# A batched row gather on Trainium2: eight resident 2 MB blocks in place of four rotating 0.5 MB buffers

## The chip, the core and the metric

The kernel runs on one core of one Trainium2 chip. The core has several engines, each with its own instruction queue: PE (matrix multiply), DVE (vector), ACT (scalar), POOL (GpSimd) and SP (sync). It has 16 DMA engines, which move data between the chip's main memory (HBM) and the core's own memory (SBUF, 128 partitions). DMAs are issued from the queues of SP, ACT and POOL. The metric is the device time of one execution in microseconds (us); lower is better.

## The reference

For each of 32 batches, 128 rows of 1024 float32 values (4 KB each) are picked out of 512 rows by an index:

```python
x = np.random.randn(32, 512, 1024).astype(np.float32)
indices = np.random.randint(0, 512, (32, 128)).astype(np.int32)

for b in range(32):
    result[b] = x[b, indices[b]]
```

Nothing is computed beyond the row addresses. 16.78 MB are read and 16.78 MB written. On the device the indices are 64-bit integers, so each one is 8 bytes long.

## The kernel before

The indices are loaded transposed, so that partition n holds index n of each of the 32 batches (L15, issued on SP). In the memory they lie batch by batch, so every element of this load is a run of 8 bytes. DVE copies the low halves of the 64-bit numbers into 32-bit ones (L17). POOL writes an iota that holds 512 b in column b (L20), and DVE adds the two (L21): column b is then the row number, in x seen as one table of 32 x 512 rows, that each partition is to fetch for batch b.

Then a loop runs over the 32 batches. POOL issues an indirect DMA (a gather, L27): partition n receives the 4 KB row that its row number names, 0.5 MB for the batch. A plain DMA stores the buffer to the output (L31), issued on SP for even batches and on ACT for odd ones. The buffers come from a pool with four slots, so gather b + 4 reuses the space of gather b, and waits until the store of batch b has landed. The framework sets all waits. It has eight semaphores for DMAs that POOL issues and eight for those of SP and ACT, used in turn; DMASW0 to DMASW7 are those of POOL's gathers in the order listings below, DMAHW0 to DMAHW7 those of loads and stores.

The order of the work on each queue is the order of the program. POOL runs 32 gathers, SP the index load and 16 stores, ACT 16 stores.

Of the kernel before, what the change touches and what calls it, by code (L numbers as in the profile page):

```python
# [5 lines left out]


@with_exitstack
def kernel(ctx, tc, x, indices, out):
    nc = tc.nc  # L10
    B, S, D = x.shape
    N = indices.shape[1]
    tp = ctx.enter_context(tc.tile_pool(name="sbuf", bufs=4))
    idx = tp.tile([128, B], dtype=indices.dtype)
    nc.sync.dma_start(out=idx[:], in_=indices[:, :].rearrange("b n -> n b"))  # L15
    idx32 = tp.tile([128, B], dtype=mybir.dt.int32)
    nc.vector.tensor_copy(out=idx32[:], in_=idx[:].bitcast(mybir.dt.int32)[:, ::2])  # L17
    idx2 = tp.tile([128, B], dtype=mybir.dt.int32)
    iota = tp.tile([128, B], dtype=mybir.dt.int32)
    nc.gpsimd.iota(iota[:], pattern=[[S, B]], base=0, channel_multiplier=0)  # L20
    nc.vector.tensor_tensor(out=idx2[:], in0=idx32[:], in1=iota[:], op=mybir.AluOpType.add)  # L21
    xf = x.flatten_outer_dims()
    of = out.flatten_outer_dims()
    engs = [nc.gpsimd, nc.sync, nc.scalar]
    for b in range(B):
        buf = tp.tile([N, D], dtype=x.dtype)
        nc.gpsimd.indirect_dma_start(  # L27
            out=buf[:], out_offset=None,
            in_=xf[:], in_offset=bass.IndirectOffsetOnAxis(ap=idx2[:, b:b+1], axis=0),
        )  # L30
        engs[1 + b % 2].dma_start(out=of[b*N:(b+1)*N], in_=buf[:])  # L31


# [1 line left out]
_INS = ['x', 'indices']  # L35
_OUTS = [((32, 128, 1024), 'float32')]


def kernel(**inputs):
    import numpy as _np  # L40
    import concourse.bacc as _bacc
    import concourse.tile as _tile
    from concourse import mybir as _mybir
    from concourse.bass_utils import run_bass_kernel_spmd as _run

    nc = _bacc.Bacc("TRN2", target_bir_lowering=False, num_devices=1)  # L46
    arrays, args = {}, []
    for name in _INS:
        a = _np.ascontiguousarray(inputs[name])
        if a.dtype.kind in "iu":  # L50
            a = a.astype(_np.int64)
        arrays[f"in_{name}_dram"] = a
        args.append(nc.dram_tensor(f"in_{name}_dram", a.shape, _mybir.dt.from_np(a.dtype), kind="ExternalInput").ap())
    for i, (shape, dtype) in enumerate(_OUTS):
        dt = _mybir.dt.from_np(_np.dtype(dtype))
        args.append(nc.dram_tensor(f"out_{i}_dram", shape, dt, kind="ExternalOutput").ap())
    with _tile.TileContext(nc) as tc:  # L57
        kernel(tc, *args)
    r = _run(nc, [arrays], core_ids=[0])
    got = tuple(r.results[0][f"out_{i}_dram"] for i in range(len(_OUTS)))  # L60
    return got[0]
```

## Time and profile before

| | |
|---|---|
| Median of 3 timed runs | 110.75 us (109.97 to 112.1) |
| Span of the profiled execution, the only time given of it | 109.6 us |
| POOL busy | 30.5 us (28%) |
| DVE busy | 0.4 us |
| Gathers (POOL, L27) | 32, 944 ns each on POOL, 6.1 us from issue to landing (median) |
| Stores (L31) | 16 on SP (5.7 us to landing), 16 on ACT (5.0 us) |
| Index load | 32 KB, 4.0 us to landing |
| Bytes through the DMA engines | 33.60 MB, 307 GB/s on average over the span |

How to read it: the busy time of POOL is what it takes to write the descriptors of the gathers; the data move later, on the DMA engines. The DMA share in a stretch is the time that packets took there, divided by 16 engines and by the length of the stretch. A packet that waits for its data counts as busy. The rate in GB/s counts a byte once for each DMA that moves it, so the 16.78 MB count twice, as gather and as store. One queue, q0, has the gathers; q1 and q10 have the DMAs of SP and ACT.

### The profile page before, as it was taken

The page shows a single profiled execution, that of the slowest core. Times are in us where ns is not written, and L with a number is a line of the kernel's source. Part 1 is how long each engine was busy: PE and PEld are TensorE (multiplying, and loading weights), DVE is VectorE, ACT ScalarE, POOL GpSimd, SP SyncE. Part 2 cuts the span into 40 slices and gives each one's busy share as a digit, 9 for nine tenths or more (in the row PEclk, how much of TensorE's full clock was granted, in tenths as well). Part 3 has the DMA queues.
Part 4 walks back from the last instruction along what each step waited for, and adds up shares of the span by engine and source line. Part 5 has one row for each costly group of instructions (what it writes and reads, how often), then busy time and mean ns, then how long its engine had stood idle before and what let it go on. Part 6 is the DMA issues. An engine that isn't in the chain of part 4 may idle for free.

```text
span 109.6 us, 173 instructions
## 1 busy us (share of the span) xinstructions
DVE 0.4 (0%) x2; POOL 30.5 (28%) x37
## 2 busy tenths in 40 slices
DVE  0100000000000000000000000000000000000000
POOL 1076002730057002730067002730037200660000
DMA  3429899899998889999998999798997999898991
GB/s 5 7 34 332 217 362 417 272 309 321 422 375 294 262 341 426 300 293 333 423 390 257 366 413 414 221 342 206 419 387 247 326 329 416 293 365 263 405 401 55
DMA packets 13329, 33.60 MB, mean 307 GB/s; under 512 B 5136, under 2 KB 5136, under 8 KB 13328
## 3 DMA queue, kind: packets, MB, share of 16 engines
q0 software_dynamic: 4608, 16.78, 48.3%
q1 hardware_dynamic: 6416, 8.42, 20.8%
q10 hardware_dynamic: 2304, 8.39, 18.7%
q14 instruction: 1, 0.01, 0.0%
HBM read 16.81 MB, written 16.78 MB: 306 GB/s over the span
## 4 chain that ended last, share of the span: by engine, by line
DMA 78%; issue 7%; POOL 2%; POOLq 1%; DVE 0%; DVEq 0%
DMA out_dram<-buf 41%; DMA buf<-in_x_dram,idx 34%; DMA idx<-in_indices_dram 4%; POOL buf L27 2%; POOLq L57 1%; DVE idx L21 0%; DVE idx L17 0%; POOLq L27 0%; DVEq L21 0%
## 5 line engine op out<-in xcount | busy, mean ns | idle before, releaser
L27 POOL DMA_INDIRECT buf<-in_x_dram,idx x32 | 30.2, 944 | 67.1 <-DMA out_dram<-buf 54.7
L20 POOL IOTA iota<- 128x32 int32 x1 | 0.1, 146 | 0.4 <-PEq L57 0.4
L17 DVE COPY idx<-idx 128x32 int32<-128x32 int32 x1 | 0.2, 181 | 4.8 <-DMA idx<-in_indices_dram 4.8
L21 DVE CUSTOM_DVE_ANT_0 idx<-idx,iota 128x64 uint16<-128x64 uint16 x1 | 0.2, 192 | 0.1
L46 POOL MEMSET const-float32-0.0<- 128x1 f32 x1 | 0.1, 99 | 0.2 <-issue 0.2
L46 POOL MEMSET const-uint8-127<- 128x1 uint8 x1 | 0.1, 119 | 0.0
L46 POOL MEMSET const-bfloat16-1.0<- 128x1 bf16 x1 | 0.1, 113 | 0.0
L46 POOL MEMSET const-float32-1.0<- 128x1 f32 x1 | 0.1, 105 | 0.0
## 6 DMA issues: line engine op xcount, KB each, us to landing
out_dram<-buf SPq DMA_DIRECT2D x16, 512.0 KB, 5.7
out_dram<-buf ACTq DMA_DIRECT2D x16, 512.0 KB, 5.0
buf<-in_x_dram,idx POOLq DMA_INDIRECT x32, 6.1
idx<-in_indices_dram SPq DMA_DIRECT2D x1, 32.0 KB, 4.0
```

Of the source, the lines that this page charges most:

```text
L17: nc.vector.tensor_copy(out=idx32[:], in_=idx[:].bitcast(mybir.dt.int32)[:, ::2])
L20: nc.gpsimd.iota(iota[:], pattern=[[S, B]], base=0, channel_multiplier=0)
L21: nc.vector.tensor_tensor(out=idx2[:], in0=idx32[:], in1=iota[:], op=mybir.AluOpType.add)
L27: nc.gpsimd.indirect_dma_start(out=buf[:], out_offset=None, in_=xf[:], in_offset=bass.IndirectOffsetOnAxis(ap=idx2[:, b:b+1], axis=0),)
L46: nc = _bacc.Bacc("TRN2", target_bir_lowering=False, num_devices=1)
L57: with _tile.TileContext(nc) as tc:
```

## The change

The batches are taken in eight blocks of four. Partition p = 32 c + q (c from 0 to 3, q from 0 to 31) handles batch 4 g + c of block g, and there the four consecutive output rows 4 q to 4 q + 3. A block is a tile of 128 partitions x 4096 floats (16 KB in each partition); the four rows lie beside each other in it. Gather k of a block fetches row 4 q + k of every partition, so one gather touches four batches, 32 rows of each. There are still 32 gathers of 0.5 MB. When the four gathers of a block have landed, one DMA stores it: 2 MB that are contiguous in the output, 16 KB from each partition. Stores alternate between SP and ACT by block. All eight blocks have a space of their own (128 KB in each partition), and none is used twice.

The index load follows the new layout: each partition reads, for each block, a run of four indices (32 bytes). The offset of the batch, 512 (4 g + c), is made from an iota, with 512/32 = 16 added from one partition to the next; a bitwise-and clears its low nine bits. One DVE instruction adds the low halves of the indices to it directly; the copy is gone.

```diff
-    tp = ctx.enter_context(tc.tile_pool(name="sbuf", bufs=4))
-    idx = tp.tile([128, B], dtype=indices.dtype)
-    nc.sync.dma_start(out=idx[:], in_=indices[:, :].rearrange("b n -> n b"))
-    idx32 = tp.tile([128, B], dtype=mybir.dt.int32)
-    nc.vector.tensor_copy(out=idx32[:], in_=idx[:].bitcast(mybir.dt.int32)[:, ::2])
-    idx2 = tp.tile([128, B], dtype=mybir.dt.int32)
-    iota = tp.tile([128, B], dtype=mybir.dt.int32)
-    nc.gpsimd.iota(iota[:], pattern=[[S, B]], base=0, channel_multiplier=0)
-    nc.vector.tensor_tensor(out=idx2[:], in0=idx32[:], in1=iota[:], op=mybir.AluOpType.add)
+    P = nc.NUM_PARTITIONS
+    K = 4
+    G = B // K
+    per = N // K
+    const = ctx.enter_context(tc.tile_pool(name="const", bufs=1))
+    rows = ctx.enter_context(tc.tile_pool(name="rows", bufs=1))
+    idx = const.tile([P, G, K], indices.dtype, name="idx")
+    nc.sync.dma_start(
+        out=idx[:], in_=indices.rearrange("(g c) (q k) -> (c q) g k", c=K, k=K)
+    )
+    ramp = const.tile([P, G * K], mybir.dt.int32, name="ramp")
+    base = const.tile([P, G * K], mybir.dt.int32, name="base")
+    nc.gpsimd.iota(
+        ramp[:], pattern=[[K * S, G], [0, K]], base=0, channel_multiplier=S // per
+    )
+    nc.vector.tensor_single_scalar(
+        out=base[:], in_=ramp[:], scalar=~(S - 1), op=mybir.AluOpType.bitwise_and
+    )
+    row = const.tile([P, G * K], mybir.dt.int32, name="row")
+    low = idx[:].rearrange("p g k -> p (g k)").bitcast(mybir.dt.int32)[:, ::2]
+    nc.vector.tensor_tensor(out=row[:], in0=low, in1=base[:], op=mybir.AluOpType.add)
     xf = x.flatten_outer_dims()
-    of = out.flatten_outer_dims()
-    engs = [nc.gpsimd, nc.sync, nc.scalar]
-    for b in range(B):
-        buf = tp.tile([N, D], dtype=x.dtype)
-        nc.gpsimd.indirect_dma_start(
-            out=buf[:], out_offset=None,
-            in_=xf[:], in_offset=bass.IndirectOffsetOnAxis(ap=idx2[:, b:b+1], axis=0),
-        )
-        engs[1 + b % 2].dma_start(out=of[b*N:(b+1)*N], in_=buf[:])
+    of = out.rearrange("(g c) (q k) d -> g (c q) (k d)", c=K, k=K)
+    for g in range(G):
+        block = rows.tile([P, K * D], x.dtype, name=f"block{g}")
+        for k in range(K):
+            c = g * K + k
+            nc.gpsimd.indirect_dma_start(
+                out=block[:, k * D:(k + 1) * D], out_offset=None,
+                in_=xf[:], in_offset=bass.IndirectOffsetOnAxis(ap=row[:, c:c + 1], axis=0),
+            )
+        eng = nc.sync if g % 2 == 0 else nc.scalar
+        eng.dma_start(out=of[g], in_=block[:])
```

What this does to POOL's queue is not in the diff, since the framework sets the waits. The order on POOL before, from the iota on, with the first gathers (the names in brackets are the semaphores that an instruction waits for):

```order
7 L20 IOTA iota_63 128x32
8 L27 DMA buf_66<-in_x_dram,idx2_62 128x1024 [waits DVE_49]
9 L27 DMA buf_69<-in_x_dram,idx2_62 128x1024
10 L27 DMA buf_72<-in_x_dram,idx2_62 128x1024
11 L27 DMA buf_75<-in_x_dram,idx2_62 128x1024
12 L27 DMA buf_78<-in_x_dram,idx2_62 128x1024 [waits DMAHW1_49,DMASW0_49]
13 L27 DMA buf_81<-in_x_dram,idx2_62 128x1024 [waits DMAHW2_49,DMASW1_49]
14 L27 DMA buf_84<-in_x_dram,idx2_62 128x1024 [waits DMAHW3_49,DMASW2_49]
```

The same place now:

```order
7 L34 IOTA ramp 128x32
8 L50 DMA block_69<-in_x_dram,row 128x1024 [waits DVE_49]
9 L50 DMA block_69<-in_x_dram,row 128x1024 x3
10 L50 DMA block_75<-in_x_dram,row 128x1024 x4
11 L50 DMA block_81<-in_x_dram,row 128x1024 [waits DMASW0_49]
12 L50 DMA block_81<-in_x_dram,row 128x1024 [waits DMASW1_49]
13 L50 DMA block_81<-in_x_dram,row 128x1024 [waits DMASW2_49]
14 L50 DMA block_81<-in_x_dram,row 128x1024 [waits DMASW3_49]
```

Before, the fifth gather is the first to wait, for a store (DMAHW1) and for the gather that filled the buffer last. Now the first eight are issued without such a wait, and the ninth waits for the first gather alone (DMASW0, whose semaphore it uses again). No gather waits for a store.

The stores on SP's queue before, after the index load:

```order
1 L15 DMA idx<-in_indices_dram 128x32x1
2 L31 DMA out_dram<-buf 128x1024 [waits DMASW0_49]
3 L31 DMA out_dram<-buf 128x1024 [waits DMASW2_49]
4 L31 DMA out_dram<-buf 128x1024 [waits DMASW4_49]
5 L31 DMA out_dram<-buf 128x1024 [waits DMASW6_49]
6 L31 DMA out_dram<-buf 128x1024 [waits DMAHW1_49,DMASW0_49]
```

And now, all of SP's DMAs:

```order
1 L27 DMA idx<-in_indices_dram 128x8x4
2 L55 DMA out_dram<-block_69 128x4096 [waits DMASW2_49,DMASW3_49,DMASW1_49,DMASW0_49]
3 L55 DMA out_dram<-block_81 128x4096 [waits DMASW2_49,DMASW3_49,DMASW1_49,DMASW0_49]
4 L55 DMA out_dram<-block_93 128x4096 [waits DMASW2_49,DMASW3_49,DMASW1_49,DMASW0_49]
5 L55 DMA out_dram<-block_105 128x4096 [waits DMASW2_49,DMASW3_49,DMASW1_49,DMASW0_49]
```

A store waited for one gather; now it waits for the four of its block. SP has four stores in place of sixteen, and ACT likewise.

## The prediction

> **What bounds the kernel now.** I read the page first, then the waits, the chain of waits, and then stretches of a few microseconds, because the page's averages mix two kinds of traffic.
>
> The page, sections 1 to 3 (engines, DMA in 40 slices, DMA queues):
>
> ```profile
> span 109.6 us, 173 instructions
> DVE 0.4 (0%) x2; POOL 30.5 (28%) x37
> DMA  3429899899998889999998999798997999898991
> GB/s 5 7 34 332 217 362 417 272 309 321 422 375 294 262 341 426 300 293 333 423 390 257 366 413 414 221 342 206 419 387 247 326 329 416 293 365 263 405 401 55
> q0 software_dynamic: 4608, 16.78, 48.3%
> ```
>
> No compute engine matters: POOL, which issues the gathers, is busy 28%. The 16 DMA engines are busy 80 to 90% of nearly every slice after the third, and yet the rate swings between 206 and 426 GB/s. So "busy" does not mean "moving at full rate". q0 carries the gathers.
>
> The waits of POOL, and the first pieces of the chain of waits (start us, us, what):
>
> ```profile
> POOL buf L27 <- DMA out_dram<-buf: 54.7, 7, 8.5
> 5.58 4.48 DMA buf<-in_x_dram,idx
> 10.06 0.02 issue
> 10.07 7.71 DMA out_dram<-buf
> 17.79 0.02 issue
> 17.81 0.02 POOLq L27
> 17.83 0.72 issue
> 18.55 5.11 DMA buf<-in_x_dram,idx
> ```
>
> There are four buffers. POOL issues four gathers, then waits until the store of the first has landed: 7 waits, 54.7 us. The chain alternates gather, store, gather. It looks like a latency problem, but POOL's idle time counts only where the DMA engines idle too. The stretches decide that. First, seven in which only gathers move (columns: stretch, length, DVE, POOL, clock, DMA share, GB/s):
>
> ```profile
> 22.00:26.00 4.00, 0.00 (x0) 0.94 (x1) 1.00 0.94 299
> 34.00:38.00 4.00, 0.00 (x0) 1.33 (x2) 1.00 0.87 296
> 47.00:51.00 4.00, 0.00 (x0) 0.92 (x1) 1.00 0.93 289
> 59.00:62.00 3.00, 0.00 (x0) 0.94 (x1) 1.00 0.86 292
> 71.00:75.00 4.00, 0.00 (x0) 1.18 (x2) 1.00 0.90 313
> 84.00:88.00 4.00, 0.00 (x0) 1.38 (x2) 1.00 0.96 333
> 96.00:100.00 4.00, 0.00 (x0) 1.88 (x2) 1.00 0.97 359
> ```
>
> Weighted by length they make 8432/27 = 312 GB/s at a mean share of 24.86/27 = 0.92. An engine that always had a gather packet would therefore work at 312/0.92 = 339 GB/s (all 16 together). Now stretches that hold only stores (18 to 20, 30 to 32, 104 to 106), and two late in a group, where stores run beside the last gather:
>
> ```profile
> 18.00:20.00 2.00, 0.00 (x0) 1.14 (x2) 1.00 0.99 404
> 30.00:32.00 2.00, 0.00 (x0) 0.94 (x1) 1.00 1.03 420
> 104.00:106.00 2.00, 0.00 (x0) 0.00 (x0) 1.00 1.01 414
> 40.00:42.00 2.00, 0.00 (x0) 0.00 (x0) 1.00 1.04 424
> 102.00:104.00 2.00, 0.00 (x0) 0.00 (x0) 1.00 1.01 416
> ```
>
> Stores alone go at about 415 GB/s, and so does a mixture. That is the point of the case: gathers alone are slow (about 312), anything with stores in it is not. And there are the worst places, at the start of a group (20 to 22, 82 to 84) and where stores have been issued but hardly move yet (12 to 14, 74 to 76):
>
> ```profile
> 20.00:22.00 2.00, 0.00 (x0) 1.68 (x2) 1.00 0.86 223
> 82.00:84.00 2.00, 0.00 (x0) 1.44 (x2) 1.00 0.71 205
> 12.00:14.00 2.00, 0.00 (x0) 0.00 (x0) 1.00 0.76 178
> 74.00:76.00 2.00, 0.00 (x0) 0.00 (x0) 1.00 0.86 188
> ```
>
> So the bound is the DMA engines' work, spoiled by low-rate stretches in every group of four.
>
> **The change, part by part.**
>
> *Head.* The index load and the ends of the span:
>
> ```profile
> q1 hardware_dynamic: 4112, 0.03, 41.4%
> 0.74 4.01 DMA idx<-in_indices_dram
> 4.78 0.19 DVE idx L17
> 5.11 0.20 DVE idx L21
> 0.00:1.80 1.80, 0.00 (x0) 0.35 (x5) 1.00 0.00 0
> 5.58:7.30 1.72, 0.00 (x0) 1.42 (x2) 1.00 0.00 0
> 108.00:109.60 1.60, 0.00 (x0) 0.00 (x0) 1.00 0.00 0
> ```
>
> The first row is the DMA view of the first 5.5 us: 4112 packets for 32 KB, nearly all of 8 bytes, keep the engines busy for 0.414 x 5.5 = 2.28 us. The new load reads runs of four indices (32 bytes), 128 x 8 = 1024 of them. At the same time for each that is 0.57 us, a saving of 1.7; the lower bound is nothing, if a 32-byte packet costs four times as much. I take 1.7, since the row's price is one of packets and not of bytes (32 KB in 2.28 us are 14 GB/s). The copy at L17 goes (5.11 - 4.78 = 0.33 us); the new bitwise-and depends only on the iota and hides under the index load (0.19 us if that cover went). First gather issue: 5.58 - 1.7 - 0.33 = 3.55. Data follow 1.72 us later: 5.3 us instead of 7.3.
>
> *Waits for the output buffer.* Each of eight blocks has its own space, so no gather waits for a store. But the order shows that a wait remains: the ninth gather and each after it waits for the gather eight places before it, whose semaphore it shares. Eight gathers stay in flight where four did. At 339 GB/s one gather lands every 0.524/339 = 1.55 us, so eight make 12 us of queue, against 4.48 us from issue to landing of the very first. Two gathers of the first group, in order of time:
>
> ```profile
> 6.97 0.94 POOL L27 DMA_INDIRECT buf<-in_x_dram,idx  x1 [0.30 <-issue]
> 8.22 0.94 POOL L27 DMA_INDIRECT buf<-in_x_dram,idx  x1 [0.30 <-issue]
> ```
>
> POOL issues one in 1.25 us, faster than one lands. The queue never runs dry; the cold starts (223, 205 GB/s) fall away after the first. With the queue full an engine that is ahead no longer waits for its neighbours, so I take 339 for gathers alone, not 312. Both ends stay for the range: 261 below, and 359, the best row, above.
>
> *Stores.* Thirty-two of 0.5 MB become eight of 2 MB, rows of 16 KB instead of 4. Each waits for four gathers. Behind a waiting store on SP or ACT stand only later stores, whose data come later anyhow; nobody else waits for them. What it costs for one store to start: the index load was issued at 0.74 us (the chain's row) and the row 0.00:1.80 shows no data until about 1.8, so 1.1 us; gathers cover that for seven of eight. For bytes I take 415 GB/s, between the two bounds 404 and 424; over the 14.7 MB of the first seven that is +0.9 or -0.8 us.
> The Trainium skill ("DMA: Bandwidth & Descriptors", Anatomy of one DMA) gives each DMA about 2.0 us fixed plus its bytes, and its Rules for kernel authors want at least 1 MiB. Twenty-four fewer stores would then save up to 48 us if each stood alone. The rows 30 to 32 and 104 to 106, with 0.5 MB stores at 420 and 414 GB/s, leave no such cost to remove: stores on two queues hide it. I take zero.
>
> *Who shares the engines.* A store row is now 16 KB; a gather row remains 4 KB. I take it that the engines alternate row by row, so that a running store has four fifths of 415 = 332 GB/s and a gather one fifth. Then stores and gathers still come in turns:
> - first block, gathers alone: 2.10/339 = 6.2 us;
> - each store: 2.10/332 = 6.3 us, in which 0.52 MB are gathered; the other 1.57 MB of the next block go alone, 1.57/339 = 4.6 us. Seven such cycles: 76.5 us;
> - the last store: nothing left to hide its start, 1.1 + 2.10/415 = 6.15 us. Before, the last store moved 0.5 MB; this longer tail is the change's own cost;
> - end of the span after the last data: 1.6 us.
>
> Sum: 5.3 + 6.2 + 76.5 + 6.15 + 1.6 = 95.7 us of span, against 109.6. The profiled execution has no time but its span; the median of the timed runs, 110.75, lies 1.1 above it, which I add: **96.8 us**.
>
> In general, with r the rate of gathers alone and 2.10 + 7 x 1.57 = 13.1 MB going alone, the time is 58.3 + 13.1/r (the 58.3 being head 5.3, seven stores 44.1, last store 6.15, end 1.6, and 1.1). At 359 GB/s it gives 94.8, at 312 100.3, at 261 108.5.
>
> **The rivals.**
>
> *B, an even mixture.* If engines alternate by equal bytes rather than by rows, a store gets half the rate and overlaps the whole next block. Then gathers are alone only in the first block: 5.3 + 6.2 + 29.4/415 (70.7) + 6.15 + 1.6 + 1.1 = 91.1 us. For it: mixed stretches already run at 424 and 416. Against: nothing of before shows a 16 KB row, so who wins a turn is open.
> The Trainium skill ("DMA: Bandwidth & Descriptors", Queues, rings and completion order) says each engine takes turns between queue rows packet by packet, and its section SWDGE vs HWDGE vs iDMA prefers packets of at most 4096 B. By that rule the turns are of equal bytes and B is what happens. No row here shows it for rows above 4 KB.
>
> *C, the gain is given back.* Gathers alone run at 240 to 261 GB/s, since the slow stretches between a store's issue and its first data are a matter of the switch and not of the buffers. By the same formula 261 gives 108.5 and 240 gives 112.9: no change. Against: seven rows between 289 and 359.
>
> *D, slower.* A deep gather queue in front of a store is itself what slows gathers. The place is the stretch between a store's issue and its first data (12 to 14: 178, 74 to 76: 188), and POOL's queue would now be eight deep there, always. At 188 GB/s it is 58.3 + 13.1/0.188 = 128 us. It decides from 240 GB/s down. For it: these stretches hold backlog and no POOL work, so lack of descriptors did not make them slow. Against: 22 to 26 and 96 to 100 have the same backlog and 299 and 359.
>
> *E, the change does not do what it says*: POOL still stalls for the gather eight places back. It does wait there, but with 12 us of work queued; it costs only if the DMA share falls between gathers. I put this within C.
>
> **How the numbers follow.** About 2% is what a measurement of this kernel can tell from no change: 108.5 to 113.0. Forecast with r from 261 up: 0.53; B: 0.22; C with E: 0.13; D: 0.12. Faster is 0.53 + 0.22 = 0.75, same 0.13, slower 0.12. The range goes from B with mixing at 424 (about 89.5) to just past the edge of the forecast, into C: 109.5. It leaves out D and most of C, about 2 in 10. The predicted time is the forecast's own, 97.
>
> **What would show it.** Head: the first gather issued near 3.6 us, index packets near 1024. No wait of POOL on out_dram. No slice below 250 GB/s between 10 and 90 us; D would show slices near 190 throughout. A against B: in A the slices swing between about 330 and 415 with gathers near a fifth of a store's stretch; in B they stand near 415 throughout and successive stores overlap. A last stretch of about 5 us with stores alone. The forecast is wrong if gathers alone stay under 261 GB/s, or if the 2 MB stores, alone, do not reach 404.

## The result and the profile after

The changed kernel takes 92.3 us (median of 4 runs, 91.6 to 92.8), against 111.4 us for the kernel before in the same comparison. The ratio is 0.834, 95% interval 0.827 to 0.841. This ratio and those below compare only the fast runs of both kernels, so they are not exactly the quotients of the medians. The forecast was 97.0 in a range of 89.5 to 109.5: the direction and the range held, and the gain was about 1.4 times the forecast's (19.1 us against 13.8).

The page of the changed kernel, sections 1 to 3 and one line of 6:

```profile
span 89.8 us, 113 instructions
DVE 0.4 (0%) x2; POOL 30.6 (34%) x37
DMA  1159999999999999999999989999999989995990
GB/s 7 7 139 321 312 367 369 412 421 436 376 418 458 421 405 423 432 434 416 411 447 425 469 358 378 467 429 387 420 494 432 431 350 414 460 445 235 467 467 0
q0 software_dynamic: 4608, 16.78, 48.2%
q1 hardware_dynamic: 1616, 8.42, 22.4%
q10 hardware_dynamic: 576, 8.39, 21.8%
block<-in_x_dram,row POOLq DMA_INDIRECT x32, 18.3
```

Two things differ from before. The DMA row is full from the fourth slice almost to the end, and the rate under it no longer falls back in every group (its lows before lay between 206 and 293); one dip, to 235, is left near the end. Also, a gather now takes 18.3 us from issue to landing where it took 6.1, and this costs nothing: it waits in a queue that does not run empty before the last gathers.

POOL's waits, and its first wait for a landing in order of time:

```profile
POOL block L50 <- DMA block<-in_x_dram,row: 26.8, 17, 4.8
3.50 1.09 POOL L50 DMA_INDIRECT block<-in_x_dram,row  x1 [2.50 <-DVE row L42]
23.79 0.94 POOL L50 DMA_INDIRECT block<-in_x_dram,row  x1 [1.79 <-DMA block<-in_x_dram,row]
```

The waits for stores are gone. The waits for the gather eight places back are there, 26.8 us in all, and harmless, as the stretches show (columns as in the prediction: stretch, length, DVE, POOL, clock, DMA share, GB/s):

```profile
5.30:16.90 11.60, 0.00 (x0) 8.86 (x10) 1.00 0.95 322
18.00:22.00 4.00, 0.00 (x0) 3.09 (x4) 1.00 0.99 420
24.00:26.00 2.00, 0.00 (x0) 1.60 (x2) 1.00 1.02 418
64.00:66.00 2.00, 0.00 (x0) 0.79 (x1) 1.00 1.02 416
16.00:82.00 66.00, 0.00 (x0) 20.66 (x22) 1.00 1.02 423
82.00:83.00 1.00, 0.00 (x0) 0.00 (x0) 1.00 0.12 49
83.00:88.20 5.20, 0.00 (x0) 0.00 (x0) 1.00 0.95 403
88.20:89.80 1.60, 0.00 (x0) 0.00 (x0) 1.00 0.00 0
```

In 5.3 to 16.9, 24 to 26 and 64 to 66 only gathers move. The first of these goes at 322 GB/s, about as the kernel before did (312); the other two at 418 and 416, as fast as a stretch in which a store runs (18 to 22). From 16 to 82 us the engines hold 423 GB/s.

Where the 19.8 us of span went can be counted from section 3 of the two pages, each queue's share times its span. Of the page before, these are the two rows that the prediction did not show:

```profile
q1 hardware_dynamic: 6416, 8.42, 20.8%
q10 hardware_dynamic: 2304, 8.39, 18.7%
```

| DMA engines' time, us (mean of the 16) | before | after | saved |
|---|---|---|---|
| gathers (q0): 48.3% of 109.6, 48.2% of 89.8 | 52.9 | 43.3 | 9.6 |
| q1 and q10 together: 39.5% and 44.2% | 43.3 | 39.7 | 3.6 |
| the rest of the span, idle | 13.4 | 6.8 | 6.6 |

In the second row the index load has 2.3 us before and 0.6 after; the stores themselves fell from 41.0 to 39.1, since a 16 KB row costs less (611 ns: 39.1 us over 64 rows for each engine) than four of 4 KB (160 ns each: 41.0 us over 256 rows). In the third row the span's two ends (without the index load) are 6.6 and 6.3, so the holes between them fell from 6.8 to 0.5. That is a little too low: packets can overlap on an engine (the share is 1.02 from 16 to 82 us), and the hole from 82 to 83 us alone is 0.9. The largest part, 9.6 us, is the same 4096 gather rows taking less engine time each.

### The profile page after: what moved, and what is told of

Its sections match the earlier page's. It is cut to its first block, busy times and chain, and to the rows that moved or that the text cites. A ratio compares the mean times of both kernels' runs of the same rounds, so it can differ in the third digit from the quotient of the medians.

```text
span 89.8 us, 113 instructions
## 1 busy us (share of the span) xinstructions
DVE 0.4 (0%) x2; POOL 30.6 (34%) x37
## 3 DMA queue, kind: packets, MB, share of 16 engines
q0 software_dynamic: 4608, 16.78, 48.2%
q10 hardware_dynamic: 576, 8.39, 21.8%
## 4 chain that ended last, share of the span: by engine, by line
DMA 44%; POOL 16%; issue 10%; POOLq 1%; DVE 0%; DVEq 0%
DMA block<-in_x_dram,row 42%; POOL block L50 16%; DMA idx<-in_indices_dram 2%; POOLq L81 1%; DVE row L42 0%; DVEq L42 0%
## 5 line engine op out<-in xcount | busy, mean ns | idle before, releaser
L50 POOL DMA_INDIRECT block<-in_x_dram,row x32 | 30.2, 944 | 33.6 <-DMA block<-in_x_dram,row 26.8
## 6 DMA issues: line engine op xcount, KB each, us to landing
block<-in_x_dram,row POOLq DMA_INDIRECT x32, 18.3
```

What stands on the lines that cost most here:

```text
L50: nc.gpsimd.indirect_dma_start(out=block[:, k * D:(k + 1) * D], out_offset=None, in_=xf[:], in_offset=bass.IndirectOffsetOnAxis(ap=row[:, ...
```

## The experiments

The question after the result was why gathers alone go at 418 GB/s in the changed kernel and at 312 in the one before, and which part of the change brings it. The theories are named in the first expectation: **depth** (enough gathers in flight), **interlude** (a running store lets the gather queue get ahead), **layout** (gathers over four batches, written 16 KB apart, are faster by themselves).

**One part alone: no waits for stores.** The kernel before, with 32 buffers:

```diff
+    bp = ctx.enter_context(tc.tile_pool(name="bufs", bufs=32))
-        buf = tp.tile([N, D], dtype=x.dtype)
+        buf = bp.tile([N, D], dtype=x.dtype)
```

> The kernel before with one edit: 32 buffers in place of 4, so no gather waits for a store; old index load, old layout, 0.5 MB stores. Three theories on why gathers alone went from about 320 GB/s to 416 after the first 17 us of the changed kernel. Depth: eight gathers in flight are enough for full rate. Interlude: it takes a stretch with a running store, in which the gather queue gets ahead of its data. Layout: gathers over four batches, written 16 KB apart, are faster by themselves. Depth and interlude: 92 to 96 us (92.3 of the changed kernel, about 2 more for the old index load, and 4 KB store rows at 159 ns each against 611 for 16 KB, 1.6 us more). Layout: 105 to 109 us, since nothing but the waits changed.

Measured: 93.96 us (93.82 to 94.08), ratio 0.857 (0.853 to 0.861). In the old code this one part brings a gain of 14.3%, where the whole change brings 16.6%. Layout is out as the cause.

**The other parts alone.** The changed kernel with its index load and its layout, but the four rotating buffers of 0.5 MB back:

```diff
-    rows = ctx.enter_context(tc.tile_pool(name="rows", bufs=1))
+    rows = ctx.enter_context(tc.tile_pool(name="rows", bufs=4))
-        block = rows.tile([P, K * D], x.dtype, name=f"block{g}")
         for k in range(K):
+            buf = rows.tile([P, D], x.dtype, name="buf")
...
-        eng.dma_start(out=of[g], in_=block[:])
+            eng.dma_start(out=of[g][:, k * D:(k + 1) * D], in_=buf[:])
```

> The changed kernel with four rotating buffers of 0.5 MB and a store after each gather, so the waits for stores are back; the new index load and the new layout stay. Depth and interlude: the old time less the head, 110.8 - 2.0 = 108.8 us, with gathers alone near 312 GB/s. Layout: gathers alone near 416, about 97 to 100 us.

Measured: 109.65 us (108.68 to 113.76), ratio 0.992 (0.984 to 1.000). POOL's waits of this kernel, and two stretches:

```profile
POOL buf L50 <- DMA out_dram<-buf: 54.5, 8, 8.1
15.00:45.00 30.00, 0.00 (x0) 9.45 (x11) 1.00 0.91 325
45.00:85.00 40.00, 0.00 (x0) 13.05 (x14) 1.00 0.94 342
```

The wait of before is back (54.5 us, it was 54.7). The first gather is issued at 3.64 us, 1.9 us earlier than before, but the interval of the ratio runs from a gain of 1.6% to none: with four buffers the new index load and the new layout are worth little, and how much of the 1.9 us arrives at the end cannot be told from this run.

**Stores of 0.5 MB instead of 2 MB**, all else as in the changed kernel:

```diff
-        eng = nc.sync if g % 2 == 0 else nc.scalar
-        eng.dma_start(out=of[g], in_=block[:])
+            eng = nc.sync if c % 2 == 0 else nc.scalar
+            eng.dma_start(out=of[g][:, k * D:(k + 1) * D], in_=block[:, k * D:(k + 1) * D])
```

> The changed kernel with one edit: each gather has its own store of 0.5 MB (4 KB rows, 16 KB apart), no buffer is used twice. If the gain comes from free buffers and a deep gather queue, 91 to 93 us: 4 KB store rows cost 1.6 us more over 16.8 MB, and stores that begin earlier save about 1.5 in the first 17 us. If it comes from the 2 MB stores or their 16 KB rows, 97 us or more. Turns by row would give a store and a gather equal shares here, about 208 GB/s each, where 16 KB rows had four fifths.

Measured: 92.40 us (92.17 to 92.43), ratio 0.842 (0.838 to 0.847), against 92.3 for the changed kernel. Only the index load and the layout separate this run from the old code with 32 buffers (93.96, the same comparison): with the waits gone they are worth 1.6 us. The block of four batches and the 2 MB store, the visible part of the change, are worth nothing that can be told here. Who gets which share of a turn cannot be read from this run, since over time gathers and stores must balance at 210 GB/s each anyhow.

**The last store cut into four.**

```diff
+            if g == G - 1:
+                eng = nc.sync if k % 2 == 0 else nc.scalar
+                eng.dma_start(out=of[g][:, k * D:(k + 1) * D], in_=block[:, k * D:(k + 1) * D])
-        eng.dma_start(out=of[g], in_=block[:])
+        if g < G - 1:
+            eng.dma_start(out=of[g], in_=block[:])
```

> The changed kernel with the store of the last block alone cut into four, each after its own gather. If the 2 MB tail is a cost by itself (6.15 us in the forecast against about 2.4 for a 0.5 MB store), about 88.5 us. If the DMA engines have work until the tail anyway, only the hole of about 1.2 us before the last store goes: 91 to 92 us, not distinguishable from 92.3.

Measured: 91.33 us (90.89 to 91.93), ratio 0.835 (0.828 to 0.842). The 2 MB tail is not a cost by itself. The same edit for the first and the last block:

> The changed kernel with the stores of the first and of the last block cut into four, each after its own gather. Stores then run in part of the first 17 us, where gathers alone made 322 GB/s against 415 to 430 with stores: up to 2.5 us less, and the hole before the last store goes (1.2 us): 89 to 91 us. If the first stretch is slow for a reason of its own (a cold queue), 91 to 92.

Measured: 91.41 us (91.09 to 91.48), ratio 0.819 (0.812 to 0.826). Against the changed kernel these edits bring at most about 1 us, nothing over 2%. The early stores did not lift the start: from 5.3 to 16.9 us the last run moves 315 GB/s, the changed kernel 322. So the time fits the second branch of that expectation; that a cold queue is the reason is not shown.

**Gathers first, then one store.** This takes the interlude away altogether, and any overlap of loads with stores too:

```diff
+    whole = rows.tile([P, G, K * D], x.dtype, name="whole")
-        block = rows.tile([P, K * D], x.dtype, name=f"block{g}")
+        block = whole[:, g, :]
-        eng.dma_start(out=of[g], in_=block[:])
+    nc.sync.dma_start(out=out.rearrange("(g c) (q k) d -> (c q) g (k d)", c=K, k=K), in_=whole[:])
```

> The changed kernel with one store of 16.8 MB in place of eight, so it starts after the last gather: gathers are alone, then the store is alone. Depth: gathers alone start near 320 GB/s and reach 416 once eight are in flight (about 28 us in); they end near 51 us, the store takes 39 (16 KB rows at 611 ns), a span of about 93 us and a time near 95. Interlude: no store runs beside the gathers, so they stay near 322; they end near 57.5 us, a span of about 99 and a time near 101.

Measured: 91.87 us (91.63 to 91.96), ratio 0.824 (0.817 to 0.831); faster than either theory said, and level with the changed kernel. Its stretches (gathers alone up to 45, the store alone from 50 on):

```profile
5.00:10.00 5.00, 0.00 (x0) 3.78 (x5) 1.00 0.86 280
10.00:15.00 5.00, 0.00 (x0) 3.78 (x5) 1.00 0.93 326
15.00:45.00 30.00, 0.00 (x0) 21.48 (x23) 1.00 1.03 419
50.00:88.00 38.00, 0.00 (x0) 0.00 (x0) 1.00 1.00 428
```

Gathers with no store beside them reach 419 GB/s from 15 us on. Interlude is out. Depth remains, but the expectation's form of it (eight in flight, from about 28 us) was wrong: full rate came earlier.

**Gathers alone, by number in flight.** Buffers rotate and only the last two are stored, so the next gather waits only for a landing (these kernels leave out most of the output, and each ran once):

```diff
-            eng = nc.sync if c % 2 == 0 else nc.scalar
-            eng.dma_start(out=of[g][:, k * D:(k + 1) * D], in_=buf[:])
+            if c >= B - 2:
+                eng = nc.sync if c % 2 == 0 else nc.scalar
+                eng.dma_start(out=of[g][:, k * D:(k + 1) * D], in_=buf[:])
```

> Gathers alone: the changed kernel's gathers into eight rotating buffers of 0.5 MB, and only the last two buffers are stored (the other stores are left out, so most of the output is not written). Eight gathers in flight. Depth: about 416 GB/s after the first 25 us, a span near 56 us. Interlude: 322 throughout, a span near 63.

> The same with four buffers, so four gathers in flight; again only the last two are stored. Depth and interlude: near 312 GB/s throughout, a span near 64 us. Layout: 416 GB/s throughout, a span near 50.

> Gathers alone with five buffers (again only the last two are stored, the rest of the output is left out). With eight buffers POOL never waited and a gather landed 6.1 us after its issue, one every 1.25 us, so about five were in flight at 420 GB/s; with four it was 336. Depth as a plain count: 5 x 0.524 MB in 6.1 + 0.3 us is 410 GB/s, so a span of 52 to 54 us, close to the 52.3 with eight buffers. If eight places are needed, a span near 58 to 60.

Measured spans: 52.3 us with eight buffers (depth's forecast was 56), 52.4 with five (52 to 54), 60.0 with four (64). Three stretches of the run with eight, then one of the run with five, then three of the one with four:

```profile
5.00:10.00 5.00, 0.00 (x0) 3.77 (x5) 1.00 0.86 281
10.00:15.00 5.00, 0.00 (x0) 3.78 (x5) 1.00 0.93 317
15.00:45.00 30.00, 0.00 (x0) 21.50 (x23) 1.00 1.03 420
```

```profile
15.00:45.00 30.00, 0.00 (x0) 21.61 (x24) 1.00 1.03 420
```

```profile
5.00:10.00 5.00, 0.00 (x0) 3.77 (x4) 1.00 0.83 268
10.00:15.00 5.00, 0.00 (x0) 2.81 (x3) 1.00 0.98 347
15.00:45.00 30.00, 0.00 (x0) 18.45 (x20) 1.00 0.96 337
```

And POOL's waits, in the order of eight buffers, then four:

```profile
POOL buf L50 <- issue: 9.5, 31, 0.3
```

```profile
POOL buf L50 <- DMA buf<-in_x_dram,row: 16.4, 27, 1.6
```

With eight buffers POOL never waits for a landing. It issues one gather in 1.25 us, and 0.524 MB in that time are 420 GB/s. The changed kernel goes no faster (416 to 418) with up to eight gathers queued, so the engines are at their limit there too. With four buffers POOL waits 27 times, 0.6 us on average, and the rate stays at 337 for good. Five are enough for the full 420. From the first issue to the last, the 31 steps take 46.9 us with four buffers and 39.2 with five, so a buffer comes round after 6.1 and 6.3 us: the round trip hardly changes, and the rate follows from how many buffers share it.

The engines are 96% "busy" at 337 GB/s too. The packet records of the traces show why. In all of these runs, the kernel before included, the median 4 KB gather packet takes 159 ns. But some packets stall: with four buffers, 6% of those after 15 us take over 200 ns, and the longest of the run 1.9 us; with five or eight buffers almost none do after 15 us. The stalled time counts as busy.

**How many buffers does the whole kernel need?** The kernel with four rotating buffers, with six and with eight:

> The kernel with four rotating buffers of 0.5 MB (new index load and layout) with six instead. Depth as a plain count: at full rate a batch takes 2 x 0.524/0.42 = 2.5 us, so six buffers allow a buffer a life of 15 us from gather to landed store; a gather needs about 6, a store 5 to 8, and POOL's restart 0.7. That is just enough or just short: 94 to 100 us. If the gain needs a buffer for each gather, 104 us or more.

> The same with eight buffers: a life of 20 us is allowed against about 12 to 14 needed. Depth as a plain count: 92 to 95 us, as good as the whole output resident. If the gain needs the whole output resident (no wait for any store), 100 us or more.

Measured: 94.97 us with six (93.58 to 95.44; ratio 0.861, 0.850 to 0.871), 92.19 with eight (92.06 to 92.46; ratio 0.834, 0.825 to 0.844). With four it was 109.65. The run with eight still waits for stores:

```profile
POOL buf L50 <- DMA out_dram<-buf: 37.9, 23, 2.9
15.00:45.00 30.00, 0.00 (x0) 11.23 (x12) 1.00 1.03 419
```

POOL waits 37.9 us in all for buffers, over a third of the span, and the engines do not notice: 419 GB/s. Eight buffers of 0.5 MB (4 KB in each partition, 32 KB in all) do what the whole output resident (128 KB) does.

## Why the prediction was right, and where its sizes were off

**Head: right.** First gather issue at 3.50 us, forecast 3.55. The index load went in 1040 packets (forecast near 1024) and landed 2.15 us after its issue instead of 4.01.

**Waits: right.** No wait for a store is left, and the wait for the gather eight places back costs nothing, because the queue behind it is full. Rival E fell.

**Who gets the turns: right.** A stretch in which the store of the first block runs beside gathers (DMA view of the changed kernel, 18 to 22 us):

```profile
q1 hardware_dynamic: 84, 1.38, 80.2%
q0 software_dynamic: 84, 0.30, 18.5%
```

A store has four fifths, as taken. The packet counts are equal, and q10's 576 packets for 8.39 MB (512 of data, 64 that signal) show that a 16 KB row is one packet. With packets of 4 KB and of 16 KB, the turns went by packet and not by bytes, so rival B's mechanism did not come. That B's 91.1 us lies nearer to the measured 92.3 than the forecast's 96.8 is luck: the gathers still went alone for long stretches, only faster. The Trainium skill ("DMA: Bandwidth & Descriptors", Queues, rings and completion order) has the turns by packet, and the trace agrees. Its preference for packets of at most 4096 B (SWDGE vs HWDGE vs iDMA) stands there with the descriptors that GpSimd writes; the prediction carried it over to stores issued on SP and ACT, and these had packets of 16 KB.

**The rate of gathers alone: mis-sized, and this is the step that failed.** The prediction took 339 GB/s, with 359, "the best row", as the upper end. It is 322 until the first store moves and 416 to 418 afterwards. With 322 for the first 2.10 MB and 417 for the other 11.0, the prediction's own formula gives 91.2 us (an estimate), so this term alone is enough to explain the gap between 96.8 and 92.3. The reason given was that engines that always have a packet lose no time to idling; the rows had been divided by their DMA share for this. But the share counted stalled packets as busy. With the deep queue the packets are shorter on average: 48.3% of 109.6 us over 256 rows for each engine is 207 ns, 48.2% of 89.8 is 169, semaphore packets included. The median is 159 ns in both traces; 515 of the 4096 gather packets took over 200 ns before, 135 after. The time above 159 ns adds up to 12.0 us for each engine before and 2.3 after, which accounts for the 9.6 us of the table. So the rows of a shallow queue were no upper bound for a deep one.

The terms show the same. The first and the last issue of stores on each queue (start, and length up to the end of the last issue):

```profile
13.32 60.85 SPq L55 DMA_DIRECT2D out_dram<-block  x4
23.63 58.96 ACTq L55 DMA_DIRECT2D out_dram<-block  x4
```

| term | forecast, us | measured, us |
|---|---|---|
| start of data and first block | 5.3 + 6.2 = 11.5 | 13.3 |
| seven cycles, up to the last store's issue | 76.5 | 68.9 (from 13.3 to about 82.3, less 0.34 for the issue itself) |
| last store | 6.15 | 5.9 |
| end | 1.6 | 1.6 |

The first block was slower than forecast by 1.8 us, the cycles faster by 7.6: 9.8 us each where 10.9 was forecast. With 0.2 us from the last store, that makes up the 5.9 us between 95.7 and 89.8.

**The longer tail as "the change's own cost": wrong in kind.** The last store's bytes must be moved at some time, and the engines were full until then. The run with one store of 16.8 MB at the end takes about the same time (91.87 us). What the tail cost here is the hole before it, 82 to 83 us above, about 1 us.

**Rivals C and D: refuted.** A deep gather queue did not slow gathers; with five or more in flight they are fast. The slow stretches that spoke for D (178, 188 GB/s) lay in groups of only four gathers. The expected swing between 330 and 415 did not show either: with gathers alone at 418 there is nothing to swing to.

**Two signs that were missed.** No slice was to fall below 250 GB/s between 10 and 90 us; the one with the hole at 82 to 83 us has 235. And the forecast was to be wrong if 2 MB stores alone did not reach 404 GB/s: the last store moves 403 from 83.0 to 88.2 us, its thin end included. The 16.8 MB store, with the same 16 KB rows, goes at 428, so the rate of stores is not what was off.

**The price of small stores: right.** Zero was taken for the 24 fewer DMAs. 0.5 MB stores in place of 2 MB cost nothing that can be told (92.40 us against 92.3), so no fixed cost for each DMA shows where the queues are full. The Trainium skill ("DMA: Bandwidth & Descriptors", Anatomy of one DMA) gives some 2 us, measured on the path of DMAs that GpSimd issues; the prediction tried it on stores of SP and ACT, and rightly did not use it.

## What to carry to other kernels

When a stream of gathers runs below the rate that stores reach on the same engines, count how many are in flight before anything else: here four of 0.5 MB were too few for gathers alone and five were enough; for gathers and stores together six buffers brought most of the gain and eight all of it. Raising that one number brought nearly all that a rewrite did. A busy DMA row is no proof of a full one, so compare its GB/s in stretches of one kind of traffic, and do not take the best rate of a starved stretch as the bound for a fed one. Once the engines were full, the order of loads and stores, the size of a store and the length of the tail no longer mattered here; only the start, the end and the holes did.

## What the runs showed of the hardware that was not expected

Gathers of 0.5 MB reach 337 GB/s with four buffers and 420 with five, and with four the engines still show 96% busy. Why some packets stall when the queue is shallow was not settled: the trace shows that they do, not which of their steps waits.

Every run with six or more buffers and the new index load also begins slowly, at 250 to 281 GB/s from 5 to 10 us and 299 to 359 from 10 to 15, and then changes to 410 or more. Depth as a plain count does not explain all of this. The queue fills slowly, since POOL issues one gather in 1.25 us. But from 10 to 13 us the run with eight buffers has 4.2 gathers in flight on average (issued, and their last packet not yet through) and moves 281 GB/s, less than the run with four buffers does later with 3.6 (337). Why the start is slower was not tested.

Loads and stores gained nothing from running beside each other: first all gathers (419 GB/s) and then one store (428) took 91.9 us, side by side at 423 took 92.3.
